# The second layer's FFN down projections as seven products instead of eight

## The chip, the cores and the metric

The kernel runs on one core of one Trainium2 chip. The metric is the device time of one execution in microseconds. Each core has five engines with queues of their own: TensorE (PE, matmuls; PEld, its weight loads), VectorE (DVE), ScalarE (ACT), GpSimd (POOL) and SyncE (SP), which here only issues DMAs. The engines wait for each other, and for transfers, through semaphores. On-chip memory is SBUF (128 partitions); matmuls write PSUM, which has eight banks of 128 x 512 f32.

## What is computed

Two layers of a decoder trunk on 512 tokens of 1024 features. In each, a normed x feeds one wide projection, four token mixers in parallel, their gated sum and an output projection; then comes the feed-forward network (FFN). The change is about the FFN, and about how x is held beside it:

```python
FFN_DIM = ((8 * D_MODEL // 3 + 255) // 256) * 256      # 2816
...
def hybrid_layer(x, ...):
    ...
    x = x + merged @ w_out
    hf = rmsnorm(x, norm_ffn)
    gate, up = jnp.split(hf @ ffn_w_up, 2, axis=-1)
    return x + (jax.nn.silu(gate) * up) @ ffn_w_down
```

All data are f32. The kernel keeps their precision with three matmuls for each product: every operand is split into a high part (rounded to the matmul's format) and a low part (the rest), and high x high, high x low and low x high are summed in PSUM (`mm3`, L267).

## The kernel before

Features are the partitions for most of the kernel: h, x and the hidden values of the FFN lie as chunks of 128 features x 512 tokens. The kernel is written on a framework that allocates buffers from pools, finds the waits itself, and orders each engine's instructions by a schedule of its own; `tc.high_priority` moves instructions forward in that order.

Weights go through `Chunk` (L212): one DMA on SyncE's queue brings up to 2048 columns into a raw buffer (`w_raw`, two of them), and halves of 1024 columns are split into `w_hi` (ScalarE, L224) and `w_lo` (VectorE, L225), three buffers each, with high priority. So a raw buffer is free once VectorE has made its last `w_lo`, and a `w_hi`/`w_lo` buffer once TensorE has done its matmuls.

`ffn` (L1052) runs in two parts, over the first six and the last five of eleven column blocks of 256. For each block, two weight chunks give two gate and two up tiles (96 matmuls of 512 columns, `features`), VectorE scales them out of PSUM (L1075), ScalarE takes the Silu, VectorE multiplies (L1080), and the product is split into `a_hi` (ScalarE) and `a_lo` (L1082). Then the part's share of the down projection follows:

- `residual` (L1014): 256 output features at a time, weights stationary, all 512 tokens moving; the sum is added to x (`xT`, held in SBUF from the mixer's end to the layer's end, L1029). In the first layer's second part it also makes the next layer's h and writes x to memory (L1033). In the second layer's first part, each finished chunk of x is transposed to token order by TensorE and copied by ScalarE (`transposed`, L1058) into `x_tok`.
- `final` (L1037): the second layer's second part, with tokens stationary and 512 columns of weights moving into four banks, one for each block of 128 tokens; VectorE adds each bank to `x_tok` (L1045) and the result goes out.

The mixer (L512) reads x back from memory at its end (L1001) and calls `residual` for the output projection (L1011). PSUM banks come from three groups: `mm` (three), `at` (two) and `tr` (three).

Of the kernel before, what the change touches and what calls it, by code (L numbers as in the profile page):

```python
# [21 lines left out]
P = 128  # L22
# [47 lines left out]
def hybrid_trunk(ctx: ExitStack, tc: tile.TileContext, x, mem, positions, norm_mix, w_in, conv_w,  # L70
# [56 lines left out]
    neg = consts.tile([P, P], F32, name="neg")  # L127
# [139 lines left out]
    def mm3(ps, a, b, first, last):  # L267
        ah, al = a
        bh, bl = b
        pe.matmul(ps, ah, bh, start=first, stop=False)  # L270
        pe.matmul(ps, ah, bl, start=False, stop=False)  # L271
        pe.matmul(ps, al, bh, start=False, stop=last)  # L272

    x_dram = nc.dram_tensor("x_spill", [P, KD, S], F32, kind="Internal").ap()
    kv_dram = [nc.dram_tensor(f"kv{l}", [P, 4, 2, 2, MEM], F32, kind="Internal").ap() for l in range(DEPTH)]
# [23 lines left out]
    def column_means(ps, ones, sq, hi, lo):  # L299
        A(hi, sq, AF.Copy)  # L300
        dve.tensor_sub(lo, sq, f(hi))
        pe.matmul(ps, ones, hi, start=True, stop=False)
        pe.matmul(ps, ones, lo, start=False, stop=True)

    def norm_feature(ssq):
        ps = tr_ps()
        column_means(ps, ones_dr, ssq, *(scratch512(S).bitcast(F32R) for _ in range(2)))
# [173 lines left out]
    ones_dr = consts.tile([P, P], F32R, name="ones_dr")  # L481
    dve.tensor_copy(ones_dr, ones_d)
# [8 lines left out]
    mx, e0, e1, sm, z0 = (small(H4, name=f"lb{i}", bufs=1) for i in range(5))  # L491
# [20 lines left out]
    def mixer(l, h, norms, cm, cf):  # L512
# [174 lines left out]
        with pool_("dsa") as dp:  # L687
# [46 lines left out]
            with pool_("idx") as ip:  # L734
# [83 lines left out]
                def select(t):  # L818
# [12 lines left out]
                    dve.copy_predicated(score[:, t * P:], future, neg)  # L831
# [23 lines left out]
                mgp = cf.enter_context(pool_("mgp", "left"))  # L855
# [142 lines left out]
        res = cf.enter_context(tc.tile_pool(name="res", bufs=1))  # L998
# [13 lines left out]
        return h2, ssq2, xT  # L1012

    def residual(xT, w2d, a, kt, cols, h2, ssq2, gain, spill=False, done=None):  # L1014
        for m0 in range(0, KD, cols // P):
            ws = []
            k0 = 0
            per = 2048 // cols
            while k0 < kt:
                n = min(per, kt - k0)  # L1020
                ws.append((k0, n, wchunk(w2d[k0 * P:(k0 + n) * P, m0 * P:m0 * P + cols], n, cols)))
                k0 += n
            pss = [mm_ps() for _ in range(cols // P)]
            for js in ([range(cols // P)] if m0 + cols // P < KD else [[j] for j in range(cols // P)]):
                for k0, n, w in ws:
                    features(w, a, js, k0, kt, [pss[j] for j in js])
            for j in range(cols // P):
                m = m0 + j
                dve.tensor_add(xT[:, m, :], xT[:, m, :], pss[j])  # L1029
                if h2 is not None:  # L1030
                    h_chunk(h2, ssq2, m, gain(m), xT[:, m, :])
                if spill:
                    nc.scalar.dma_start(x_dram[:, m, :], xT[:, m, :])  # L1033
                if done is not None:
                    done(m)

    def final(x_tok, w2d, a, kt):  # L1037
        for m0 in range(0, D, 512):
            cols = slice(m0, m0 + 512)
            ws = [wchunk(w2d[k0 * P:min(k0 + 4, kt) * P, cols], min(4, kt - k0), 512) for k0 in range(0, kt, 4)]  # L1040
            pss = [mm_ps() for _ in range(MM_BUFS)] + [at_ps()]
            tokens_wide(ws, a, kt, pss)
            for t, ps in enumerate(pss):
                for c in ([cols] if m0 == 0 else [slice(m0 + e, m0 + e + 256) for e in (0, 256)]):
                    dve.tensor_add(x_tok[:, t, c], x_tok[:, t, c], ps[:, c.start - m0:c.stop - m0])  # L1045
                    if m0:
                        q = nc.sync if c.start == m0 else nc.scalar
                        q.dma_start(out[0][t * P:(t + 1) * P, c], x_tok[:, t, c])
            if m0 == 0:
                nc.sync.dma_start(out[0][:, cols].rearrange("(t p) c -> p t c", p=P), x_tok[:, :, cols])  # L1050

    def ffn(l, h, ssq, xT):  # L1052
# [5 lines left out]
        def transposed(m):  # L1058
            ps = tr_ps()
            for t in range(NT):  # L1060
                pe.transpose(ps[:, t * P:(t + 1) * P], xT[:, m, t * P:(t + 1) * P], ident)
            A(x_tok[:, :, m * P:(m + 1) * P], ps.rearrange("p (a b) -> p a b", b=P), AF.Copy)

        with tc.tile_pool(name="ffn", bufs=1) as fp:
            for f0, f1 in parts:
                kt = 2 * (f1 - f0)
                a = (fp.tile([P, 12, S], F32R, name="a_hi")[:, :kt], fp.tile([P, 12, S], F32R, name="a_lo")[:, :kt])
                for fc in range(f0, f1):
                    wg = wchunk(ffn_w_up[l][:, fc * 256:(fc + 1) * 256], KD, 256)
                    wu = wchunk(ffn_w_up[l][:, FF + fc * 256:FF + (fc + 1) * 256], KD, 256)  # L1070
                    gs = [fp.tile([P, S], F32, name="fg", bufs=2) for _ in range(2)]
                    us = [fp.tile([P, S], F32, name="fu", bufs=2) for _ in range(2)]
                    for w, dsts in ((wg, gs), (wu, us)):
                        for dst, ps in zip(dsts, features(w, h, (0, 1))):
                            dve.tensor_mul(dst, ps, r_b)  # L1075
                    for j in range(2):
                        i = 2 * (fc - f0) + j
                        g, u = gs[j], us[j]
                        A(g, g, AF.Silu)
                        dve.tensor_mul(g, g, u)  # L1080
                        A(a[0][:, i, :], g, AF.Copy)
                        dve.tensor_sub(a[1][:, i, :], g, f(a[0][:, i, :]))  # L1082
                wd = ffn_w_down[l][f0 * 256:f1 * 256, :]
                h2 = ssq2 = None
                if last and f1 == n_f:
                    final(x_tok, wd, a, kt)
                    continue
                if f1 == n_f:
                    h2, ssq2 = new_h(), new_ssq()
                if last:  # L1090
                    x_tok = fp.tile([P, NT, D], F32, name="x_tok")
                residual(xT, wd, a, kt, 256, h2, ssq2, lambda c: g_mix(l + 1, c), spill=h2 is not None,
                         done=transposed if last else None)
        return h2, ssq2

    for l in range(DEPTH):
        with ExitStack() as ctx_ffn:
            with ExitStack() as ctx_mix:
                h, ssq, xT = mixer(l, h, (lambda: (norm_token(ssq), norm_feature(ssq))) if l else (lambda: norms),
                                   ctx_mix, ctx_ffn)  # L1100
            h, ssq = ffn(l, h, ssq, xT)
# [29 lines left out]
```

## Time and profile before

| | us |
|---|---|
| median of three runs (2047.14 to 2047.64) | 2047.41 |
| the profiled execution | 2046.88 |
| its span, from the first to the last instruction | 2044.9 |
| ScalarE busy in the span | 1022.0 |
| first matmul on the second layer's hidden values | 1808.48 |
| first matmul of `final` | 1986.36 |
| start of the last matmul | 2040.54 |

How to read it: the page gives each engine's busy time and its share of the span, 40 slices of the span with the busy share in tenths and the clock granted to TensorE, the chain of waits (followed back from the last instruction to what released each step), and groups of like instructions with their count, mean duration and the idle time ahead of them. Stretch views give the same sums for chosen times. A matmul's shown duration (some 390 ns) is longer than the pitch at which matmuls follow each other, since they are pipelined.

### The profile page before, as it was taken

To read this page: it belongs to the slowest core of one execution; us is meant where nothing else is said; L and a number is where in the kernel's file an instruction comes from. 1 tells how busy PE (TensorE), PEld (TensorE's weight loads), DVE (VectorE), ACT (ScalarE), POOL (GpSimd) and SP (SyncE) were. 2 spreads that over 40 slices of the span, in tenths; PEclk is the share of its full clock that TensorE was granted. 3 is DMA by queue.
4 is the path that set the end of the run, shared out by engine and by line. 5 is a ranking of instruction groups with operands and counts; after the bars stand their busy time and mean duration, and the time that the engine had idled before them with its cause. 6 is when DMAs were issued, how large, how long until landed. Compare 5 with 4: busy or idle time off the path is not lost.

```text
span 2044.9 us, 26596 instructions
## 1 busy us (share of the span) xinstructions
PE 2032.3 (99%) x10348; PEld 1714.7 (84%) x10348; DVE 1274.7 (62%) x2519; ACT 1022.0 (50%) x1844; POOL 9.8 (0%) x33
## 2 busy tenths in 40 slices
PE   8999999999999999999999999999999999999999
PEld 8998988888888888888889898888888788888887
DVE  6779998547676544334457889953777654533442
ACT  7653655766665423223355466576766633322231
POOL 0000000000000000000000000000000000000000
PEclk9999999999999999999999999999999999999999
DMA  7623222223233232232243213322222423323222
GB/s 253 219 88 94 68 93 93 64 71 93 83 113 114 87 100 92 93 110 97 88 155 94 88 59 112 93 73 63 83 83 83 144 89 97 103 73 112 93 83 93
DMA packets 187709, 203.79 MB, mean 100 GB/s; under 512 B 4271, under 2 KB 176385, under 8 KB 187457
## 3 DMA queue, kind: packets, MB, share of 16 engines
q1 hardware_dynamic: 183296, 193.04, 29.7%
q10 hardware_dynamic: 4128, 8.93, 1.2%
q8 instruction: 81, 1.33, 0.3%
q14 instruction: 44, 0.35, 0.1%
q0 software_dynamic: 160, 0.13, 0.0%
HBM read 191.60 MB, written 10.49 MB: 99 GB/s over the span
## 4 chain that ended last, share of the span: by engine, by line
PE 98%; DMA 1%; ACT 1%; DVE 1%; issue 0%; SPq 0%; DVEq 0%
PE mm L270 30%; PE mm L271 29%; PE mm L272 29%; PE tr L726 1%; PE tr L720 1%; PE at L697 1%; PE at L696 1%; PE at L272 1%; PE at L270 1%; PE at L271 1%; DMA w_raw<-in_mem_w_kv_dram 1%; PE at L974 0%; PE at L948 0%; PE tr L664 0%; PE tr L765 0%; PE tr L631 0%
## 5 line engine op out<-in xcount | busy, mean ns | idle before, releaser
L270 PE MATMUL mm<-h_hi,w_hi 128*128 128x512 f32 x1664 | 652.0, 393 | 1.0 <-DVE fg L1075 0.4
L225 DVE TENSOR_TENSOR w_lo<-w_raw,w_hi 128x1024 fp32r<-128x1024 f32 (+1 forms) x346 | 419.7, 1214 | 372.3 <-ACT w_hi L97 371.9
L271 PE MATMUL mm<-h_lo,w_hi 128*128 128x512 f32 x1664 | 651.5, 392 | 0.0
L272 PE MATMUL mm<-h_hi,w_lo 128*128 128x512 f32 x1664 | 649.1, 391 | 0.0
L97 ACT ACTIVATE w_hi<-w_raw 128x1024 fp32r<-128x1024 f32 (+1 forms) x346 | 363.3, 1051 | 452.5 <-PE mm L271 406.1
L270 PEld LDWEIGHTS mm<-h_hi,w_hi 128*128 128x128 f32 x1664 | 312.7, 188 | 66.0 <-DVE fg L1075 1.2
L272 PEld LDWEIGHTS mm<-h_hi,w_lo 128*128 128x128 f32 x1664 | 312.6, 188 | 64.2 <-issue 0.2
L271 PEld LDWEIGHTS mm<-h_lo,w_hi 128*128 128x128 f32 x1664 | 312.8, 188 | 63.0 <-issue 1.0
L272 PE MATMUL mm<-w_hi,h_lo 128*128 128x256 f32 (+1 forms) x448 | 128.2, 286 | 0.0
L271 PE MATMUL mm<-w_lo,h_hi 128*128 128x256 f32 (+1 forms) x448 | 127.0, 284 | 0.0
L270 PE MATMUL mm<-w_hi,h_hi 128*128 128x256 f32 (+1 forms) x448 | 127.0, 285 | 0.0
L271 PE MATMUL mm<-a_lo,w_hi 128*128 128x512 f32 x272 | 106.3, 391 | 0.0
L270 PE MATMUL mm<-a_hi,w_hi 128*128 128x512 f32 x272 | 106.0, 390 | 0.0
L272 PE MATMUL mm<-a_hi,w_lo 128*128 128x512 f32 x272 | 105.7, 391 | 0.0
L270 PE MATMUL mm<-y_hi,w_hi 128*128 128x512 f32 x256 | 100.7, 395 | 1.2 <-ACT y_hi L97 1.2
L272 PE MATMUL mm<-y_hi,w_lo 128*128 128x512 f32 x256 | 100.4, 392 | 0.0
L271 PE MATMUL mm<-y_lo,w_hi 128*128 128x512 f32 x256 | 100.3, 392 | 0.0
L272 PEld LDWEIGHTS mm<-w_hi,h_lo 128*128 128x128 f32 x448 | 85.7, 191 | 1.4 <-issue 0.8
L270 PEld LDWEIGHTS mm<-w_hi,h_hi 128*128 128x128 f32 x448 | 85.3, 191 | 1.2 <-issue 0.8
L271 PEld LDWEIGHTS mm<-w_lo,h_hi 128*128 128x128 f32 x448 | 85.6, 191 | 0.6
L97 ACT ACTIVATE a_hi<-fg 128x512 fp32r<-128x512 f32 x44 | 27.8, 633 | 106.8 <-DVE fg L1080 106.8
L97 ACT ACTIVATE prob<-prob,small 128x128 f32<-128x128 f32 (+3 forms) x128 | 69.2, 555 | 15.2 <-DVE small L709 14.6
(370 smaller groups left out, 2958.1 us busy)
## 6 DMA issues: line engine op xcount, KB each, us to landing
w_raw<-in_w_in_dram SPq DMA_DIRECT2D x72, 1024.0 KB, 5.3
w_raw<-in_ffn_w_up_dram SPq DMA_DIRECT2D x44, 1024.0 KB, 5.1
w_raw<-in_w_lift_dram SPq DMA_DIRECT2D x32, 512.0 KB, 3.4
w_raw<-in_ffn_w_down_dram SPq DMA_DIRECT2D x16, 1024.0 KB, 5.4
w_raw<-in_mem_w_kv_dram SPq DMA_DIRECT2D x8, 1024.0 KB, 5.2
w_raw<-in_w_out_dram SPq DMA_DIRECT2D x8, 1024.0 KB, 5.3
w_raw<-in_ffn_w_down_dram SPq DMA_DIRECT2D x10, 512.0 KB, 3.4
kv<-kv ACTq DMA_DIRECT2D x8, 512.0 KB, 6.4
```

The source lines that it names most:

```text
L97: i = act.activation(dst, src, func, **kw)
L225: dve.tensor_sub(lo, raw[:, k:e], f(hi))
L270: pe.matmul(ps, ah, bh, start=first, stop=False)
L271: pe.matmul(ps, ah, bl, start=False, stop=False)
L272: pe.matmul(ps, al, bh, start=False, stop=last)
L696: pe.matmul(ps, q[:, hh, s], k[0][:, :n], start=True, stop=False)
L697: pe.matmul(ps, q[:, hh, s], k[1][:, :n], start=False, stop=True)
L720: pe.transpose(pp[:, (2 * e + i) * P:(2 * e + i + 1) * P], probs[2 * i + e][:, b * P:(b + 1) * P], ident)
L726: pe.matmul(pv[e * HD:(e + 1) * HD, :], vt[:, b, :], pt[:, b, e * 2 * P:(e + 1) * 2 * P], start=b == 0, stop=b == t)
```

## The change

The second layer's down projection is written as a block product with one block fewer. For each pair of hidden chunks (K = 2 x 128), the hidden values are cut into halves by K (the two chunks g0, g1) and by tokens (256 each), and the weights by K and by columns (`C2` = 0:512, `C1` = 512:1024). Seven products of quarter size, whose operands are sums and differences of quarters, replace eight; some stand in several results, and the banks are added to the accumulator `acc` (x in token order) several times.

- `operands` makes from g0 and g1 seven half-token tiles, high and low, for all pairs of a part (six buffers each).
- `down` runs four loops over the pairs. The first and second use four banks; `ba` goes on accumulating over all four loops, `bb` restarts with the second. The second loop makes two differences of weights on VectorE and writes one of them to memory (`t2_spill`, on ScalarE's queue); the fourth reads it back. `evict`, with twice the priority offset of the splits, adds banks to `acc` between the loops.
- `raw_tile` gives every third raw weight tile a third buffer (`w_raw7`).
- The first layer's down projection keeps its eight products (`add_down`), but x isn't held in SBUF: `residual` always writes its chunks to memory, and the FFN fetches them one by one on GpSimd's queue (`x_chunk`) and, in the first layer, writes them back after each part. In the second layer the fetched chunks are transposed during the up projections of blocks 1 to 4 (`x_in`).
- Smaller edits: `neg` has one column and is broadcast, one matrix of ones is dropped and its factor goes into `column_means`, five small tiles share a ring, x and the merged branches leave SBUF with the mixer, the FFN's pool waits tile by tile for reused memory, and `mm3` can pass a flag.

```diff
-    neg = consts.tile([P, P], F32, name="neg")
+    neg = consts.tile([P, 1], F32, name="neg")
...
-    def column_means(ps, ones, sq, hi, lo):
-        A(hi, sq, AF.Copy)
-        dve.tensor_sub(lo, sq, f(hi))
+    def column_means(ps, ones, sq, hi, lo, scale=1.0):
+        A(hi, sq, AF.Copy, scale=scale)
+        dve.scalar_tensor_tensor(lo, sq, scale, f(hi), op0=OP.mult, op1=OP.subtract)
...
+    def add_down(x_chunk, w2d, a, kt, h2, ssq2, gain):
+        for m0 in range(0, KD, 2):
...
+            xs = [x_chunk(m0 + j) for j in range(2)]
...
+            for j, xc in enumerate(xs):
+                m = m0 + j
+                dve.tensor_add(xc, xc, pss[j])
                 if h2 is not None:
+                    h_chunk(h2, ssq2, m, gain(m), xc)
+                nc.scalar.dma_start(x_dram[:, m, :], xc)
...
+    def raw_tile(fp, turn=[0]):
+        turn[0] += 1
+        if turn[0] % 3 == 0:
+            return fp.tile([P, 2048], F32, name="w_raw7")
+        return wpool.tile([P, 2048], F32, name="w_raw", bufs=RAW_BUFS)
+
+    def split(src):
...
+        with tc.high_priority(offset=AHEAD):
+            A(hi, src, AF.Copy)
+            dve.tensor_sub(lo, src, f(hi))
...
+    def operands(fp, g0, g1):
...
+        put(A11, 1, g0[:, :HALF])
+        put(A12, 2, g1)
+        dve.tensor_add(g0[:, HALF:], g0[:, HALF:], g1[:, HALF:])
+        dve.tensor_sub(g0[:, :HALF], g0[:, HALF:], g0[:, :HALF])
+        both = g1.rearrange("p (a b) -> p a b", b=HALF)
+        dve.tensor_sub(both, both, g0[:, None, :HALF].to_broadcast([P, 2, HALF]))
+        put(S2, 2, g0)
+        put(S4, 2, g1)
+        return hi, lo
+
+    def down(fp, w2d, ops, spill, evict):
...
+        ba, bb = [mm_ps(), mm_ps()], [b0, at_ps()]
...
+        for i0 in range(0, n, 2):
...
+            nc.sync.dma_start(raw, w2d[2 * i0 * P:2 * (i0 + m) * P, C1].rearrange("(k p) n -> p k n", p=P))
+            for i in range(m):
+                p1, p2 = split(raw[:, 2 * i:2 * i + 2, :])
+                prod(ba, i0 + i, A11, p1, i0 + i == 0, i0 + i == n - 1)
+                prod(bb, i0 + i, A12, p2, i0 + i == 0, i0 + i == n - 1)
+        evict(ba, 0, C1, 0)
+        evict(bb, 0, C1, 1)
+        for i in range(n):
+            raw = raw_tile(fp)[:, :1536]
+            nc.sync.dma_start(raw[:, :1024], w2d[2 * i * P:(2 * i + 1) * P, :])
+            nc.sync.dma_start(raw[:, 1024:], w2d[(2 * i + 1) * P:(2 * i + 2) * P, C2])
+            with tc.high_priority(offset=AHEAD):
+                dve.tensor_sub(raw[:, 512:1024], raw[:, :512], raw[:, 512:1024])
+                dve.tensor_sub(raw[:, 1024:], raw[:, 1024:], raw[:, 512:1024])
+            p5, p6 = split(raw[:, 512:].rearrange("p (k n) -> p k n", n=512))
+            nc.scalar.dma_start(spill[:, i, :], raw[:, 1024:])
+            prod(ba, i, S2, p6, False, i == n - 1, True)
+            prod(bb, i, S1, p5, i == 0, i == n - 1)
+        evict(ba, 0, C2, 0)
+        evict(bb, 2, C2, 0)
+        for i0 in range(0, n, 2):
...
+            with tc.high_priority(offset=AHEAD):
+                dve.tensor_sub(raw[:, 0::2, :], raw[:, 1::2, :], raw[:, 0::2, :])
+            for i in range(m):
+                p7, p3 = split(raw[:, 2 * i:2 * i + 2, :])
+                prod(ba, i0 + i, S3, p7, False, i0 + i == n - 1, True)
+                prod(bb, i0 + i, S4, p3, False, i0 + i == n - 1, True)
+        evict(ba, 2, C2, 1)
+        evict(bb, 0, C2, 1)
+        for i0 in range(0, n, 2):
...
+            nc.sync.dma_start(raw[:, :m, :], rows[:, i0:i0 + m, 1, C1])
+            nc.sync.dma_start(raw[:, m:, :], spill[:, i0:i0 + m, :])
+            with tc.high_priority(offset=AHEAD):
+                dve.tensor_sub(raw[:, :m, :], raw[:, :m, :], raw[:, m:, :])
+            for i, p4 in enumerate(split(raw[:, :m, :])):
+                prod(ba, i0 + i, A22, p4, False, i0 + i == n - 1, True)
+        evict(ba, 2, C1, 0)
...
+            def x_chunk(m):
+                xc = fp.tile([P, S], F32, name="x_c", bufs=2 if last else 4)
+                nc.gpsimd.dma_start(xc, x_dram[:, m, :])
+                return xc
...
+                    ops.append(operands(fp, *gs))
+                    if fc == 0:
+                        acc = fp.tile([P, NT, D], F32, name="acc")
+                    if 0 < fc < 5:
+                        x_in(2 * fc - 2)
+                        x_in(2 * fc - 1)
...
+                def evict(bank, t0, cols, times):
+                    tail = final and t0 and cols is C1
+                    with tc.high_priority(offset=2 * AHEAD):
+                        for t, ps in enumerate(bank):
+                            for w in (slice(0, 256), slice(256, 512)) if tail else (slice(0, 512),):
+                                c = slice(cols.start + w.start, cols.start + w.stop)
+                                d = acc[:, t0 + t, c]
+                                dve.tensor_add(d, d, ps[:, w])
```

More of the change, by code (lines that the diff above doesn't have):

```diff
@@ L490, in hybrid_trunk @@
     a0, a1 = prm[:, 64:68], prm[:, 68:72]
-    mx, e0, e1, sm, z0 = (small(H4, name=f"lb{i}", bufs=1) for i in range(5))
+    mx, e0, e1, sm, z0 = (small(H4) for _ in range(5))
     dve.tensor_max(mx, a0, a1)
@@ L1029, in residual @@
                 dve.tensor_add(xT[:, m, :], xT[:, m, :], pss[j])
-                if h2 is not None:
[L1031 to L1050, printed above, removed]
@@ L1094, in ffn @@
+                down(fp, wd, ops, t2_dram[:, part], evict)
         return h2, ssq2
     for l in range(DEPTH):
[L1097 to L1101, printed above, removed]
+        with ExitStack() as ctx_mix:
+            h, ssq = mixer(l, h, (lambda: (norm_token(ssq), norm_feature(ssq))) if l else (lambda: norms), ctx_mix)
```

127 lines of the change are left out of this document (80 added, 47 removed).

## The prediction

> **What bounds the kernel now.** First the page's head: how long the span is, which engine fills it, and whether its clock is whole.
>
> ```profile
> span 2044.9 us, 26596 instructions
> ...
> PE 2032.3 (99%) x10348; PEld 1714.7 (84%) x10348; DVE 1274.7 (62%) x2519; ACT 1022.0 (50%) x1844; POOL 9.8 (0%) x33
> ...
> PEclk9999999999999999999999999999999999999999
> ...
> PE 98%; DMA 1%; ACT 1%; DVE 1%; issue 0%; SPq 0%; DVEq 0%
> PE mm L270 30%; PE mm L271 29%; PE mm L272 29%; PE tr L726 1%; PE tr L720 1%; PE at L697 1%; PE at L696 1%; PE at L272 1%; PE at L270 1%; PE at L271 1%; DMA w_raw<-in_mem_w_kv_dram 1%; PE at L974 0%; PE at L948 0%; PE tr L664 0%; PE tr L765 0%; PE tr L631 0%
> ```
>
> TensorE is busy 99% of the span and is 98% of the chain of waits; its idle time in all is 2044.9 - 2032.3 = 12.6 us. So a matmul left out is worth its full pitch, and any new wait of TensorE costs its full length. The pitch comes from the stretch view over the second layer's last down projection (`final`, 240 matmuls), and the stretch before it shows the up projections.
>
> ```profile
> 1911.00:1985.00 74.00, 74.00 (x328) 61.27 (x327) 34.44 (x41) 22.06 (x27) 0.00 (x0) 1.00 0.28 90
> ...
> 1986.30:2040.95 54.65, 54.62 (x241) 1.00 0.23 78
> ```
>
> The columns are length, then busy time and count of TensorE, of its weight loads, VectorE, ScalarE and GpSimd (the second row is TensorE alone), granted clock, DMA share, GB/s. 54.65 / 241 = 0.2268 us per matmul of 512 columns, with no hole. VectorE is 47% busy in the up projections, ScalarE 30%: that is the cover for what the change adds.
>
> **The matmuls removed.** Before, the second layer's down projections are 8 x 12 x 3 = 288 matmuls (part of six pairs of K chunks) and 2 x 4 x 10 x 3 = 240 (part of five): 528. After, each pair takes seven products x 2 token blocks x 3 = 42, times 11 pairs: 462. In the built program TensorE's matmuls go from 10071 to 10005, the same 66 fewer. 66 x 0.2268 = **-15.0 us**, certain as long as TensorE is fed. The 32 transposes of x stay (they move from the down to the up projections), and so do the eight copies out of PSUM, so these moves are 0.
>
> **What is put in their place.** The durations, from the groups over the second layer's FFN and from VectorE's timeline:
>
> ```profile
> L225 DVE TENSOR_TENSOR w_lo<-w_raw,w_hi 128x1024 fp32r<-128x1024 f32 x60 | 73.5, 1225 | 126.6 <-ACT w_hi L97 126.6
> L97 ACT ACTIVATE w_hi<-w_raw 128x1024 fp32r<-128x1024 f32 x60 | 63.7, 1061 | 139.5 <-PE mm L271 111.2 <-PE at L272 19.8 <-PE mm L272 8.5
> ...
> L97 ACT ACTIVATE a_hi<-fg 128x512 fp32r<-128x512 f32 x21 | 13.3, 633 | 52.9 <-DVE fg L1080 52.9
> ...
> L1045 DVE TENSOR_TENSOR x_tok<-x_tok,mm 128x256 f32<-128x256 f32 x6 | 2.3, 418 | 11.1 <-PE mm L272 11.1
> L1045 DVE TENSOR_TENSOR x_tok<-x_tok,mm 128x512 f32<-128x512 f32 x3 | 2.0, 683 | 0.6 <-PE mm L272 0.6
> ```
>
> ```profile
> 1942.44 0.69 DVE L1082 TENSOR_TENSOR a_lo<-fg,a_hi 128x512 fp32r<-128x512 f32 x1 [0.70 <-ACT a_hi L97]
> 1943.05 0.69 DVE L1075 TENSOR_TENSOR fu<-mm,rstd 128x512 f32<-128x512 f32 x1
> 1943.96 1.22 DVE L225 TENSOR_TENSOR w_lo<-w_raw,w_hi 128x1024 fp32r<-128x1024 f32 x1 [0.23 <-ACT w_hi L97]
> 1945.10 0.68 DVE L1080 TENSOR_TENSOR fg<-fg,fu 128x512 f32<-128x512 f32 x1
> ```
>
> Back to back on VectorE a 512-wide subtraction takes 0.61 us (1942.44 to 1943.05) and a 1024-wide one 1.14 (1943.96 to 1945.10); a split of 1024 columns is 1.06 on ScalarE and then 1.14 on VectorE. In the up projections `operands` replaces two 512-wide subtractions by four and three 256-wide ones: 4 x 0.61 + 3 x 0.42 - 2 x 0.61 = +2.5 us per 96 matmuls (21.8 us), 11% more on a VectorE that is 47% busy; ScalarE gets about 1.0 more (633 ns a copy): hidden, 0. If that cover were gone, the projections' banks would be emptied late and up to 2.5 us per step would show.
>
> In the down projections I call the four loops of `down` passes 1 to 4. A tile is one pair's weights (1024 columns, 12 matmuls, 2.72 us; in pass 4, two pairs). With six pairs the passes are 72, 72, 72 and 36 matmuls. VectorE has, in pass 2, 12 new 512-wide subtractions (7.3), six splits (6.8) and four accumulator additions (2.4) = 16.6 us against 16.3 us of matmuls; over all four passes about 50 us against 57. So it is not the bound by amount, but it is full in pass 2, and it takes its instructions in the order that the scheduler wrote. What decides is when each raw buffer is filled. The transfers:
>
> ```profile
> w_raw<-in_ffn_w_down_dram SPq DMA_DIRECT2D x16, 1024.0 KB, 5.4
> w_raw<-in_ffn_w_down_dram SPq DMA_DIRECT2D x10, 512.0 KB, 3.4
> ...
> xT<-x_spill SPq DMA_DIRECT2D x16, 256.0 KB, 5.2
> ...
> mv<-kv SPq DMA_DIRECT2D x8, 256.0 KB, 3.0
> ...
> x_spill<-xT ACTq DMA_DIRECT2D x8, 256.0 KB, 6.2
> ```
>
> ```profile
> 10.00:15.00 5.00, 3.08 (x17) 1.98 (x18) 4.04 (x15) 4.23 (x11) 0.00 (x0) 0.97 1.04 408
> 15.00:20.00 5.00, 5.00 (x32) 5.00 (x32) 2.62 (x13) 4.84 (x11) 0.00 (x0) 0.69 1.08 360
> ...
> 1595.00:1600.00 5.00, 3.83 (x16) 2.47 (x14) 2.87 (x5) 1.14 (x2) 0.00 (x0) 1.00 0.00 0
> ```
>
> A pass 2 tile loads 512 + 256 KB and spills 256 KB: 1.05 MB per 2.72 us is 385 GB/s, while the busiest stretch of the trace moved 408. There are three raw buffers; one is free again when its split is done and its spill has landed. No row has 768 KB: between 3.4 and 5.4 I take 3.4 for the first transfer and 4.4 for both. A 256 KB spill lands in 3.0 us (the kv row, alone) to 6.2 (the x_spill row, beside weight loads).
>
> **The waits, worked through the built order.** Clock 0 is the end of the first part's up projections. VectorE still has the last pair's operands to make, and waits in between for pass 2's first raw buffer, whose subtractions stand among them; the split of pass 1's fourth tile so ends at about 8.5 and of the sixth at 11.4. Only these free the buffers of pass 2's second and third tiles: loaded at 12.0/12.9 and 14.9/15.8, their four subtractions end at 16.5, the second tile's split at 17.6, and only behind it in VectorE's order stands the first accumulator addition (18.3). TensorE is done with pass 1 at 72 x 0.2268 = 16.3 and adds pass 2 onto that same bank: **it waits 2.0 us**. Behind the waiting matmul stands the rest of TensorE's queue, and nothing else can use the time.
>
> Going on in the same way: the split of pass 2's fourth tile stands behind the sixth tile's subtractions, so behind the third buffer's spill and load: 0.2 us (spill 3.0) to 1.9 (spill 6.2). Pass 2 to 3: the first buffer of pass 3 (1 MB, 5.4) is subtracted ahead of the additions, and its split behind two of them: 1.8 to 2.4. Pass 3 to 4: the addition stands behind the third buffer's subtraction: 1.5. First part: 5.5 to 7.8. Second part (five pairs): its additions stand one split earlier, 0.7; pass 2, 0.3; pass 2 to 3, with the split behind all four additions, 2.4 to 5.0; pass 3 to 4, 0.1. That is 3.5 to 6.1. Together 9.0 to 13.9. I take **+10.5**, nearer the lower end because a spill of pass 2 meets loads of 768 KB, a good part of which have landed by then, where the 6.2 row meets 1 MB loads.
>
> The bounds of this cost: below, if the additions never wait for a transfer, each boundary costs the two additions that TensorE cannot run beside, 0.7 us at most, so about 4; above, if both loads take the 5.4 row and every spill the 6.2 row, each of the seven waits grows by another 1.0: 13.9 + 7 = 20.9.
>
> **The clock.** At 15 to 20 us the granted clock is 0.69, after stretches in which TensorE was idle 1.9 us of 5; at 1595 to 1600 it idled 1.17 us and kept 1.00. My waits of 0.7 to 2.4 us lie between these, so I cost the clock at 0 and keep a rival for it: by the row at 15 us every wait might be charged. The Trainium skill, page "TensorE: Matmul & The Clock Gate", section "HAM oscillation — how this bites in real kernels", says that idle gaps of more than about 3.4 us halve the clock. By that rule only a wait at the upper end of the longest one (5.0 us) would be charged, and an estimate from the page's window of 3.4 us at half speed is 1.7 us on the sum.
>
> **First layer, and the rest.** `add_down` fetches x in chunks on GpSimd's queue and writes them back on ScalarE's. A fetch is at most 5.2 us and the write before it 6.2; four buffers let it start one step of 72 matmuls (16.3 us) ahead: hidden, 0. Without that cover each of the eight steps would wait up to 5.2. The 24 further writes of x and 11 spills are issued on ScalarE, which is half idle. `norm_feature`, the narrower `neg` and the pools change no count of instructions on the path. The scheduler also reorders the mixers; the idle time of the whole trace, 12.6 us, shows that little can be won there, and I take 0, with 3 us either way. The end is alike: a last matmul, two 256-wide additions, two transfers.
>
> **Sum.** 2044.9 - 15.0 + 10.5 = 2040.4 span. The profiled run took 2046.88, 2.0 more than its span, which gives 2042.4; the median of the runs shown, 2047.41, lies 0.5 above the profiled run, so **2042.9 us**.
>
> **Rivals.**
> Cover holds: raw buffers come in time, waits of about 4 to 6 us, 2047.4 - 15.0 + 5 = 2037.4. For it: 385 GB/s lies under the 408 that a stretch reached, and VectorE has 7 us to spare. Against: the order puts additions behind work that waits for transfers.
> All given back: spills always at 6.2 and some waits longer, 15 us: 2047.4.
> Slower: the ring of three raw buffers sets the pace of pass 2. Place: VectorE at `down`'s two subtractions, for a buffer whose spill has not landed. Price: the upper bound, 20.9 us, 2047.4 - 15.0 + 20.9 = 2053.3. It decides once load plus spill takes more than about 10 us in the mean, so that the waits exceed 15. For it: the 5.4 and 6.2 rows; against: three buffers, and only three tiles of each pass 2 need a buffer that has just been spilled.
> The clock: each of seven waits costs a spell like that at 15 to 20 us, 0.31 x 5 = 1.55: 7 x 1.55 = 10.9 more, 2053.8. Against it: the 1.17 us hole that cost nothing.
> That the products are not saved at all can be left out: the built order has them.
>
> **How the numbers follow.** A measurement of this kernel can tell about 0.2% (4.1 us) from no change: faster is below 2043.3, slower above 2051.5. The forecast (waits of 7 to 14 us, 2039 to 2046.5) has 0.50, cover holds 0.20, all given back 0.09, the ring 0.16, the clock 0.05. Faster: 0.20 and 0.30 of the forecast's 0.50, whose centre lies just under the bound: 0.50. Slower: the ring and the clock, 0.21. Same: the rest, 0.29. The range reaches from the second rival's lower waits (2036) to the ring (2053); the forecast's own is 2039 to 2046.5.
>
> **What would show it.** Right: TensorE shows 66 matmuls fewer and in each part three holes, the longest at the changes of pass, ended by an accumulator addition or a split on VectorE; the pitch stays 0.227; DMA over 300 GB/s in pass 2; up projections and first layer without new holes. The sum of holes sets the time: about 10 us. Wrong: holes in the first layer ended by x chunks, a granted clock under 1.00 in the passes, or pass 2 stretched evenly (the ring).

## The result, and the profile after

| | before | after |
|---|---|---|
| median, us | 2047.36 (2047.14 to 2047.64, 4 runs) | 2056.01 (2054.34 to 2056.84, 4 runs) |
| the profiled execution's span | 2044.9 | 2052.6 |
| last matmul of the second mixer's output projection starts | 1676.70 | 1683.05 |
| first part of the down projection, first to last matmul | 67.89 | 65.20 |
| second part | 54.17 | 56.01 |

The ratio is 1.0041, 95% interval 1.0029 to 1.0053: slower, by 8.6 us in the medians and 7.7 in the spans. The page of the changed kernel, its head, chain of waits and the down projections' weight loads:

```profile
span 2052.6 us, 26852 instructions
...
PE 2030.9 (99%) x10282; PEld 1703.5 (83%) x10282; DVE 1353.0 (66%) x2634; ACT 1047.7 (51%) x1883; POOL 22.6 (1%) x57
...
PE 93%; DMA 3%; DVE 2%; ACT 1%; issue 1%; SPq 0%; DVEq 0%; ACTq 0%
...
w_raw<-in_ffn_w_down_dram SPq DMA_DIRECT2D x18, 1024.0 KB, 5.5
...
w_raw<-in_ffn_w_down_dram SPq DMA_DIRECT2D x22, 512.0 KB, 4.7
```

TensorE has 66 instructions fewer but is busy only 1.4 us less, where 66 x 0.2268 would be 15.0; its share of the chain falls from 98% to 93%, and what took its place is mostly transfers (1% to 3%) and VectorE (1% to 2%). So there are two losses: matmuls that became slower, and waits. The stretch view of the changed kernel finds the place of each (columns as in the prediction: length, busy and count by engine, granted clock, DMA share, GB/s). The rows are the first layer's FFN, the second layer's first up projections, the 192 matmuls of its output projection on `mg` (the merged mixers' outputs, high and low part), and the two parts of its down projection:

```profile
702.70:1044.00 341.30, 341.12 (x1505) 282.12 (x1504) 151.36 (x178) 104.29 (x125) 6.94 (x13) 1.00 0.36 113
...
1684.50:1812.00 127.50, 127.50 (x580) 105.91 (x579) 71.50 (x95) 50.16 (x69) 3.22 (x6) 1.00 0.37 121
1638.48:1683.05 44.57, 44.57 (x192) 35.85 (x191) 25.56 (x32) 17.47 (x23) 1.06 (x2) 1.00 0.42 137
1817.92:1883.12 65.20, 59.26 (x252) 46.33 (x251) 50.84 (x59) 23.51 (x24) 0.00 (x0) 1.00 0.67 225
1992.15:2048.16 56.01, 51.03 (x210) 39.38 (x209) 42.25 (x53) 17.99 (x19) 0.00 (x0) 0.97 0.62 205
```

The same view of the kernel before, for the same 192 matmuls:

```profile
1633.41:1676.70 43.29, 43.29 (x192) 35.87 (x191) 25.42 (x32) 17.51 (x23) 0.00 (x0) 1.00 0.26 88
```

Both rows are full of matmuls, without a hole, at the whole clock, and yet one takes 1.28 us longer: from first to last start 44.57 / 191 = 233.4 ns a matmul against 43.29 / 191 = 226.7. The matmuls with `y` (one mixer's output, ahead of the merging) as the moving operand slowed too, from 228 to 233 ns start to start in the mean, and no other large group of 512 columns did. With both layers' mixers that comes to 1683.05 - 1676.70 = 6.35 us, all of it ahead of any product that the change leaves out.

The down projections, first to last start, take 65.20 us where 251 pitches of 0.2267 are 56.90, and 56.01 where 209 are 47.38: waits of 8.30 and 8.63 us. What ended TensorE's waits in the first part, from the view of waits (total, times, longest):

```profile
PE mm L270 <- DVE acc L1202: 3.9, 2, 2.3
PE mm L271 <- DVE w_lo L1058: 1.3, 3, 0.5
PE mm L270 <- ACT w_hi L97: 0.7, 1, 0.7
```

and in the second:

```profile
PE mm L270 <- ACT w_hi L97: 4.1, 3, 2.0
PE mm L270 <- DVE acc L1202: 0.6, 2, 0.4
PE mm L271 <- DVE w_lo L1058: 0.2, 1, 0.2
```

In the first part the accumulator additions end most of the waiting, in the second the splits of weights that are late. After the longest wait of the second part the granted clock is half for one window (0.97 in the stretch view), about 1.6 us. The balance: -15.0 for the matmuls, +6.35 ahead, +16.9 in the passes, about -0.6 in small things, is the +7.7 of the spans.

### The profile page after: what moved, and what is told of

Same layout as the page of the kernel before. It is cut to its first block, busy times and chain, and to the rows that moved or that the text cites. A ratio compares the mean times of both kernels' runs of the same rounds, so it can differ in the third digit from the quotient of the medians.

```text
span 2052.6 us, 26852 instructions
## 1 busy us (share of the span) xinstructions
PE 2030.9 (99%) x10282; PEld 1703.5 (83%) x10282; DVE 1353.0 (66%) x2634; ACT 1047.7 (51%) x1883; POOL 22.6 (1%) x57
## 4 chain that ended last, share of the span: by engine, by line
PE 93%; DMA 3%; DVE 2%; ACT 1%; issue 1%; SPq 0%; DVEq 0%; ACTq 0%
PE mm L270 28%; PE mm L271 28%; PE mm L272 28%; DMA w_raw<-in_ffn_w_down_dram 2%; PE tr L725 1%; PE tr L719 1%; PE at L696 1%; DVE w_lo L1058 1%; PE at L695 1%; DMA w_raw<-in_mem_w_kv_dram 1%; ACT w_hi L97 0%; PE at L272 0%; PE at L271 0%; PE at L270 0%; PE tr L663 0%
## 5 line engine op out<-in xcount | busy, mean ns | idle before, releaser
L97 ACT ACTIVATE w_hi<-w_raw 128x1024 fp32r<-128x1024 f32 (+1 forms) x363 | 380.5, 1050 | 443.0 <-PE mm L271 354.5
L225 DVE TENSOR_TENSOR w_lo<-w_raw,w_hi 128x1024 fp32r<-128x1024 f32 (+1 forms) x324 | 392.4, 1212 | 296.1 <-ACT w_hi L97 295.5
L97 ACT ACTIVATE a_hi<-fg 128x512 fp32r<-128x512 f32 (+1 forms) x66 | 39.4, 597 | 113.9 <-DVE fg L1174 97.4
L270 PE MATMUL mm<-a_hi,w_hi 128*128 128x512 f32 x176 | 68.5, 389 | 0.0
L271 PE MATMUL mm<-a_lo,w_hi 128*128 128x512 f32 x176 | 68.5, 389 | 0.0
L272 PE MATMUL mm<-a_hi,w_lo 128*128 128x512 f32 x176 | 68.0, 389 | 0.0
```

The costliest lines, as they stand in the source:

```text
L97: i = act.activation(dst, src, func, **kw)
L225: dve.tensor_sub(lo, raw[:, k:e], f(hi))
L270: pe.matmul(ps, ah, bh, start=first, stop=False, skip_group_check=more)
L271: pe.matmul(ps, ah, bl, start=False, stop=False, skip_group_check=more)
L272: pe.matmul(ps, al, bh, start=False, stop=last, skip_group_check=more)
```

## The experiments

Waits below are, as above, the first-to-last length of a part less its pitches (56.90 and 47.38). A hole is the distance between two matmul starts less one pitch, and a boundary is the change from one pass (one of the four loops of `down`) to the next.

**The slow matmuls.** The small edits take 1152 bytes out of the constants, so the weight parts and h, which lie behind them, move: in the built programs `w_hi` starts at byte 80992 before and 79840 after, 96 and 224 modulo 256. `y` and `mg` are laid out from the other end of memory and stay at 96 modulo 256. Theory A is that this difference slows them. First the changed kernel with one tile more:

```diff
+        shift = mix.tile([P, 32], F32, name="shift")
+        pool.memset(shift, 0.0)
         res = cm.enter_context(pool_("res", "left"))
```

> The changed kernel with 128 bytes more in the mixers' pool, ahead of the lifted outputs' buffers, so that y and mg lie at the same byte address modulo 256 as the weight parts again (both 224; in the changed kernel 96 beside 224, in the kernel before 96 beside 96). Theory A, that a moving operand whose address differs from the stationary one's by 128 modulo 256 makes the matmul slower: the 576 matmuls per layer on y and mg go back from about 233 ns to 227 ns, start to start; 2 x 576 x 5.7 ns = 6.5 us, so the time is about 2049.5 us and the second FFN begins about 6.3 us earlier than in the changed kernel. Rival B, that the slower matmuls come from other work on the memories at that time (transfers of the first layer put on another queue, VectorE writes), or from their order: 2056 us, pitch still 233 ns.

Measured: 2046.73 us (2045.58 to 2048.91), ratio to the kernel before 0.9998, interval 0.9990 to 1.0007. The stretch view, the `mg` row and the two parts:

```profile
1632.72:1676.02 43.30, 43.30 (x193) 35.86 (x191) 25.45 (x32) 17.50 (x23) 1.08 (x2) 1.00 0.42 141
1810.87:1874.22 63.35, 58.93 (x252) 46.41 (x251) 50.87 (x59) 23.51 (x24) 0.00 (x0) 1.00 0.68 231
1983.25:2040.36 57.11, 52.51 (x211) 40.60 (x209) 42.31 (x53) 17.96 (x19) 0.00 (x0) 0.94 0.61 201
```

The matmuls on `mg` take 43.30 us again, with the changed kernel's transfers beside them (0.42 DMA share as in the changed kernel), so it is neither traffic nor order. The projection ends 7.0 us earlier than in the changed kernel (1676.02 against 1683.05); with the first part 1.85 shorter and the second 1.1 longer (by two windows of half clock in place of one), that makes the 7.8 by which the spans differ. Why the parts changed with it is open. The medians differ by 9.3, more than the 6.5 that A had; the changed kernel's profiled run (2054.34) was the fastest of its four. Then the other direction, the kernel before with two of the small edits:

```diff
-    neg = consts.tile([P, P], F32, name="neg")
+    neg = consts.tile([P, 1], F32, name="neg")
...
-    mx, e0, e1, sm, z0 = (small(H4, name=f"lb{i}", bufs=1) for i in range(5))
+    mx, e0, e1, sm, z0 = (small(H4) for _ in range(5))
...
-                    dve.copy_predicated(score[:, t * P:], future, neg)
+                    dve.copy_predicated(score[:, t * P:], future, neg.to_broadcast([P, P]))
```

> The kernel before with two of the small edits alone: the constant neg as one column, and the five lb tiles in the ring of small tiles. The down projections stay plain. The left pools move down by 640 bytes, so the weight parts go from 96 to 224 modulo 256, and y and mg stay at 96. Theory A (addresses): the matmuls on y and mg go from 227 to 233 ns, and the time rises by about 6.3 us to 2053.7. Rival B (other work or the order): within 1 us of 2047.4. Rival C, that the broadcast of neg itself costs something in the selection: the rise stands in the selections, with the pitch of y and mg unchanged.

Measured: 2053.16 us, ratio 1.0028 (1.0017 to 1.0038). The `mg` row:

```profile
1638.36:1682.93 44.57, 44.57 (x192) 35.85 (x191) 25.57 (x32) 17.48 (x23) 0.00 (x0) 1.00 0.25 84
```

The length is that of the changed kernel to the hundredth, and its end lies 6.2 us later than before. Two edits that save 640 bytes and no instruction cost 5.7 us. B falls, and so does C, which had the pitch unchanged. Last, the matmul alone:

> Not the kernel, but its matmul alone: the output is only a copy of x, and all the reference's computation is left out. Stationary tiles of 128x128 and moving tiles of 128x512, FP32R, three matmuls a step as in the kernel, on one core; the stationary side at an address 0 or 128 bytes on, the moving side at 0, 32, 64 ... 480 bytes on, 24 matmuls for each of the 32 pairs; first with nothing else running, then a second time while ScalarE, VectorE and DMA write and read all the while. Theory A (the difference of the two addresses modulo 256 sets the pitch): about 226.5 ns where the difference is 0, about 233 ns where it is 128, with a period of 256, the same for both stationary positions once the difference is taken, quiet or not. Rival A2 (the moving address alone): the slow offsets are the same for both stationary positions. Rival A3 (it is contention with other engines' accesses): no difference in the quiet sweep, one in the second.

The stretch view, one row for 24 matmuls, from the first start of one pair of addresses to that of the next:

```profile
25.37:30.81 5.44, 5.44 (x25) 4.51 (x24) 0.00 (x0) 0.00 (x0) 0.00 (x0) 1.00 0.00 0
30.81:36.42 5.61, 5.61 (x26) 4.50 (x25) 0.00 (x0) 0.00 (x0) 0.00 (x0) 1.00 0.01 3
...
47.53:53.13 5.60, 5.60 (x25) 4.50 (x24) 0.00 (x0) 0.00 (x0) 0.00 (x0) 1.00 0.00 0
136.97:142.43 5.46, 5.46 (x25) 4.50 (x24) 0.00 (x0) 0.00 (x0) 0.00 (x0) 1.00 0.00 0
...
292.94:298.54 5.60, 5.60 (x26) 4.51 (x25) 5.43 (x6) 5.41 (x7) 0.00 (x0) 1.00 1.09 347
315.35:320.82 5.47, 5.47 (x26) 4.50 (x24) 5.30 (x6) 5.31 (x6) 0.00 (x0) 1.00 1.08 347
```

These are, in order: moving less stationary address 0, 32 and 128 bytes with the stationary side at 0; 0 with the stationary side at 128; and there once more, while the other engines and 347 GB/s of transfers run, 128 and 0. The sixteen moving offsets, for each stationary position and with or without traffic, give the same pitch at the same difference modulo 256, within 1 ns:

| difference modulo 256, bytes | 0 | 32 | 64 | 96 | 128 | 160 | 192 | 224 |
|---|---|---|---|---|---|---|---|---|
| ns a matmul | 227 to 228 | 233.5 | 229.3 | 233.9 | 233.5 | 234 | 233.5 | 233.1 |

A holds; the moving address alone (A2) and contention (A3) fall.

**The waits.** The first idea was VectorE's order:

```diff
+    def behind(i, made):
+        for m in made:
+            tc.add_manual_dep(i.ins, m.name, order, reason="additions first")
...
-        evict(ba, 0, C1, 0)
+        made = evict(ba, 0, C1, 0)
...
-                dve.tensor_sub(raw[:, 512:1024], raw[:, :512], raw[:, 512:1024])
+                i1 = dve.tensor_sub(raw[:, 512:1024], raw[:, :512], raw[:, 512:1024])
+                behind(i1, made if i > 1 else [])
```

and so at the other two boundaries.

> The changed kernel with an order given to VectorE at the three boundaries of each down projection: the subtractions of the next pass, from its second tile of weights on (third pass: from the first; fourth: from the second), are issued behind the additions that free the first pair of accumulators. No instruction is added or taken away. Theory D, that the holes at the first and the third boundary (2.50 and 1.72 us in part 1, 1.54 in part 2) come from subtractions ahead of the additions on VectorE: these fall to under 1 us each, the total of the waits in the two parts from 16.9 to about 13 us, and the time to about 2052.5. Rival E, that the transfers alone decide (the weights are late whatever the order): the hole only moves to the next split, and the time stays within 0.7 us of 2056.

Measured: 2058.98 us, ratio 1.0059 (1.0046 to 1.0071): slower. TensorE's waits in the first part:

```profile
PE mm L270 <- ACT w_hi L97: 2.4, 1, 2.4
PE mm L270 <- DVE acc L1210: 2.2, 3, 1.0
PE mm L271 <- DVE w_lo L1058: 1.7, 1, 1.7
```

The additions now cost 2.2 instead of 3.9 (first boundary 2.50 to 2.06 in two pieces, third 1.72 to 0.59), but the second boundary, whose subtractions were put back, grew from 1.6 to 4.4. Two windows of half clock came in each part. The waits are 10.6 and 12.2; without the clock (four windows, 1.6 each) 16.4, where the changed kernel has 15.3. In the second part the third boundary's hole, which D had under 1 us, grew from 1.5 to 2.0, and one inside the second pass from 0.9 to 2.1. D falls for the three boundaries together, and E's form, "the hole only moves", holds; that the clock would make it dearer was in neither.

> Both edits together. If A and D hold and add up: about 2046, below the kernel before by about 1.4 us. If only A holds: 2049.5; only D: 2052.5; neither: 2056.

Measured: 2052.60 us (1.0015 to 1.0033): A's gain (6.4 against e3) and e3's loss (5.9 against e1) add up. That it is the number expected for "only D" is chance: A holds here, and the order costs time.

Then what the weights are late for. Without the writes of t2:

```diff
-            nc.scalar.dma_start(spill[:, i, :], raw[:, 1024:])
...
-            nc.sync.dma_start(raw[:, m:, :], spill[:, i0:i0 + m, :])
+            nc.sync.dma_start(raw[:, m:, :], rows[:, i0:i0 + m, 1, C2])
```

> The changed kernel without the writes that put the second pass's combinations (t2) into DRAM; the fourth pass reads as many bytes of the weights in their place, so what is subtracted there is not what the reference needs. Theory R (the holes from the second pass to the third come from the three raw buffers: each is held until its t2 write has landed, and the next load stands behind it on SP): the loads of the third pass are issued earlier, the hole at that boundary falls from 2.18 to under 1 us in part 2 and from 1.6 to under 0.8 in part 1, no window of half clock follows, and the waits of part 2 go from 8.6 to about 5 us. Rival V (VectorE has too much in front of the split): the holes stay within 0.5 us of what they were. The hole from the first pass to the second (2.50 us in part 1) changes in neither.

Measured in one run: 2055.32 us; waits 8.2 and 9.2, with a window of half clock in each part. Without these two, 14.2 are left of 15.3. In the second part the hole of 2.18 became 0.72 and another of 3.2 three matmuls later, so it moved; R's 5 us for this part and its whole clock did not come, and V's unchanged holes did not either. In the changed kernel the weight loads of the third pass (L1119) waited mostly for t2 writes, from the view of waits of SP's queue over the second part:

```profile
SPq L1205 <- DVE acc L1202: 18.3, 8, 6.2
SPq L1105 <- DVE w_lo L1058: 11.5, 3, 10.4
SPq L1119 <- DMA t_spill<-w_raw: 10.8, 3, 6.5
```

and without these writes, for splits:

```profile
SPq L1105 <- DVE w_lo L1058: 22.4, 5, 10.4
SPq L1204 <- DVE acc L1201: 16.6, 6, 5.7
SPq L1130 <- DVE w_lo L1058: 12.9, 3, 8.1
SPq L1118 <- DVE w_lo L1058: 6.7, 3, 2.6
```

The write was the last thing to hold a buffer, not the only one. (The largest line of the first view, output writes that wait for additions, is no cause here: the load behind them, at 2011.62, still had 0.9 us to wait for a t2 write.) Without the weight subtractions (L1108, L1109, L1121 and L1134 left out):

> The changed kernel without its four kinds of weight subtractions on VectorE (some 20 to 24 instructions of 0.69 to 1.23 us a part); the passes multiply the weights as loaded, so the output is another. Loads, writes and splits stay. Theory V: VectorE's amount of work makes the holes, so those at the first and the third boundary fall from 2.50, 1.72 and 1.54 to under 0.5 us, that at the second from 2.18 to under 1.2, and the waits of the two parts from 16.9 to under 7 us in all. Theory R: the boundary from the second pass to the third still has a hole of at least 1.5 us in part 2, because its load stands behind the t2 write, and the waits stay over 10 us in all.

Measured in one run: 2047.72 us, with no window of half clock in the two parts:

```profile
1818.24:1878.92 60.68, 57.70 (x252) 46.89 (x251) 36.87 (x42) 23.62 (x24) 0.00 (x0) 1.00 0.72 241
1987.95:2041.57 53.62, 48.80 (x210) 38.84 (x209) 30.36 (x37) 18.00 (x19) 0.00 (x0) 1.00 0.64 214
```

That is waits of 3.8 and 6.2, in all 10.0 where V said under 7 and R over 10. In the first part the first and third hole are 0.54 each, about what V has, and the second boundary has 2.37, more than the 1.6 of the changed kernel; in the second part 1.49 inside the second pass, 2.11 at the second boundary and 1.37 at the third are left. So without VectorE's subtractions some 5 us of the 15.3 go, most of them in the first part, and the rest stays. Last, more buffers, where the memory has room for them: in the second part h is read no more, and two raw tiles can lie there.

```diff
-    def raw_tile(fp, turn=[0]):
+    def raw_tile(fp, extra, turn=[0]):
         turn[0] += 1
-        if turn[0] % 3 == 0:
+        n = turn[0] % (5 if extra else 3)
+        if n == 0:
             return fp.tile([P, 2048], F32, name="w_raw7")
+        if n > 2:
+            return f(state.tile([P, KD, S], F32R, name=("h_hi", "h_lo")[n - 3], bufs=1)[:, :4]).rearrange(
+                "p a b -> p (a b)")
```

> The changed kernel with the 128 bytes (as in e1) and, in the second part's down projection alone, five raw buffers in place of three: the two further ones lie where h was, which nothing reads any more. No other instruction is changed. Theory R: in part 2 the holes inside the second pass and at the second boundary, 9.4 us of waits and slow clock with e1, fall to about 3 us (what the accumulators cost at the boundaries), and the time from 2046.7 to about 2041, under the kernel before; part 1 stays at 6.4 us. Rival T (the transfers' rate decides, 218 GB/s moved there already): the loads are issued earlier but land as late, and the time is within 1 us of 2046.7. Rival V (VectorE): the same, the splits come no earlier.

Measured: 2043.09 us (2042.41 to 2045.07), ratio 0.9980 (0.9971 to 0.9990). The two parts:

```profile
1811.49:1876.49 65.00, 60.39 (x253) 47.67 (x252) 51.01 (x60) 23.40 (x24) 0.00 (x0) 0.97 0.66 229
1985.51:2036.95 51.44, 48.66 (x211) 38.76 (x209) 40.50 (x51) 17.66 (x19) 0.00 (x0) 1.00 0.60 213
```

The second part's waits fall from 9.7 (57.11 in e1) to 4.1; of these 5.7, 3.2 are the two windows of half clock that are gone, and 2.5 are waits. The holes inside the second pass, at the second and at the third boundary are 0.8, 0.55 and 0.54, and the one at the first grew from 0.6 to 1.55. Of the gain of 5.7 the time keeps 3.6, since a window of half clock fell into the first part here; R had 2041. Where the weights come from shows on SP's queue. In the changed kernel the last load of the second pass (L1105) and the first of the third (L1119) are issued at

```profile
2011.62 0.34 SPq L1105 DMA_DIRECT2D w_raw<-in_ffn_w_down_dram  x1
2012.01 0.46 SPq L1106 DMA_DIRECT2D w_raw<-in_ffn_w_down_dram  x1
2015.99 0.38 SPq L1119 DMA_DIRECT2D w_raw<-in_ffn_w_down_dram  x1
```

The last lands some 5.7 us later, VectorE subtracts at 2021.80, and TensorE, out of work at 2022.3, goes on at 2024.31. With five buffers (the second pass ends 6.7 us earlier here) they go out at

```profile
1996.21 0.33 SPq L1111 DMA_DIRECT2D h_hi<-in_ffn_w_down_dram  x1
...
1997.95 0.38 SPq L1125 DMA_DIRECT2D h_lo<-in_ffn_w_down_dram  x1
```

which is 18 us ahead of the end of the second pass (2015.6), not 6. T and V had the time within 1 us of 2046.7, and it is 3.6 lower; the passes go faster, at 213 GB/s where e1 had 201. So neither is what makes these holes. R holds with a correction: it is the number of buffers, not the t2 write alone, that makes the loads late.

With the weights early, the order can help at the one boundary where nothing is late behind it:

```diff
-        evict(ba, 2, C2, 1)
+        made = evict(ba, 2, C2, 1)
...
-                dve.tensor_sub(raw[:, :m, :], raw[:, :m, :], raw[:, m:, :])
+                i1 = dve.tensor_sub(raw[:, :m, :], raw[:, :m, :], raw[:, m:, :])
+                for e in made if i0 > 2 else []:
+                    tc.add_manual_dep(i1.ins, e.name, order, reason="additions first")
```

> The kernel of e8 with the order on VectorE at one boundary only: the fourth pass's subtractions, from its second tile on, stand behind the additions that free the accumulators of its first products. In e3, where all three boundaries were ordered, this one fell from 1.72 to 0.59 us in part 1. Theory D4 (here nothing is late behind it, since the fourth pass has half the products of the others on PE... and its loads are early): part 1's hole at the third boundary falls from 1.73 to about 0.6, part 2's stays at 0.54, and the time falls by about 1 us, to 2042. Rival E (the work only moves): a new hole of about 1 us inside the fourth pass of part 1, and the time within 0.4 us of 2043.1.

> The kernel of e8 once more, beside e9 on the same chip. In e8 one window of half clock fell into part 1, behind the hole of 2.4 us between its first and second pass (56% of that window idle), where e1 had none at 55%. If that is the place of the window boundary in the run and nothing of the kernel, a profile of this kernel may be without it, and part 1 then takes 63.3 us as in e1 in place of 65.0; the median stays at 2043.1 within 0.7 us.

Measured: e9 2041.71 us, ratio 0.9973 (0.9963 to 0.9984); e8's kernel again 2042.83, 0.9979 (0.9971 to 0.9988), with a window of half clock in the first part again. e9's parts:

```profile
1811.91:1874.74 62.83, 58.76 (x252) 46.49 (x251) 51.18 (x59) 23.51 (x24) 0.00 (x0) 1.00 0.71 238
1983.77:2035.64 51.87, 48.93 (x210) 38.76 (x209) 40.51 (x51) 17.67 (x19) 0.00 (x0) 1.00 0.62 211
```

The third boundary's hole in the first part fell from 1.73 to 0.59 as D4 said, and no hole came inside the fourth pass; one inside the second grew from 0.2 to 1.0, and the second part is 0.5 longer than in e10. So 0.7 of the 1.1 us gained at the boundary is lost inside the second pass, where neither D4 nor E had it. The medians differ by 1.1 us, but the intervals of the ratios overlap, and the profile's 2.2 us in the first part are partly the missing clock window. e9 is the fastest kernel here, 5.5 us under the one before and 14.3 under the changed one.

## Why the prediction was wrong

It said 2042.9 with a range of 2036 to 2053; the result is 2056.0. Its steps:

- **Matmuls removed, -15.0: right.** 10348 to 10282 instructions, and the passes' pitch stayed at 0.2267.
- **Up projections and `operands` hidden, transposes 0, first layer 0: right.** The rows at 1684.50 (127.50 of 127.50 us busy) and 702.70 (341.12 of 341.30, before 340.60 of 340.80) have no new holes. The end after the last matmul is 4.4 us in both.
- **The failed step: "change no count of instructions on the path ... and I take 0, with 3 us either way".** That the count stays was right; that a matmul's pitch stays with it was assumed. The edits moved addresses, and 1152 matmuls ahead of the down projections lost 5.5 ns each, 6.35 us, twice the allowance. e1 and e2 show that this is the cause, in both directions. Nothing in the trace of before announced it, but the addresses could have been compared.
- **The second failed step: waits, +10.5, "nearer the lower end".** They were right in kind and too small: 15.3, and 1.6 of half clock:

| boundary | said, part 1 | measured | said, part 2 | measured |
|---|---|---|---|---|
| first to second pass | 2.0 | 2.5 | 0.7 | 0.9 |
| inside the second | 0.2 to 1.9 | 0.7 | 0.3 | 1.1 |
| second to third | 1.8 to 2.4 | 1.6 | 2.4 to 5.0 | 2.4 |
| third to fourth | 1.5 | 1.7 | 0.1 | 1.5 |

 The first part's boundaries were right within 0.5. The second part's were too short inside the second pass and at the third boundary, both ended by splits: I let the buffers there come in time. The reason given for the lower end was that the loads beside a t2 write have in good part landed by then. In the second part the three loads of the third pass (at 2015.99, 2017.28 and 2024.28) waited for t2 writes issued at 2011.05, 2012.38 and 2017.84, which puts these writes at 4.9, 4.9 and 6.4 us, in the upper half of the 3.0 to 6.2 that I had or over it. (The one write of the first part whose landing the trace shows took 3.2; the kv row that I took 3.0 from is a read.) The two loads of a tile were right in the first part (4.4 for both, measured from 1830.42 to 1834.80), but of three tiles asked for within 3.3 us in the second (from 2000.48) two had their second load landing 6.4 and 7.4 us after its issue. The rest, some 2.9 us, is a split of the first pass (0.4) that I did not have and many small pieces, among them about 0.1 us more for the first matmul after each hole.
- **The clock at 0: wrong by 1.6.** It fell to half behind one wait of 2.02 us. So a granted clock under 1.00 in the passes, one of the prediction's signs of being wrong, came. The rule quoted from the Trainium skill, page "TensorE: Matmul & The Clock Gate", section "HAM oscillation — how this bites in real kernels", by which gaps over about 3.4 us do that, does not agree with this: the gap was shorter. Its rival, a charge for each of seven waits, was wrong too.
- **The rivals.** The ring of three raw buffers was the nearest. e8 shows its mechanism in the second part, where two buffers more take 5.7 us off, 3.2 of them clock; its price of 20.9 was too high, and its place (the t2 write) was not the only one, by e6. "DMA over 300 GB/s in pass 2" was not reached: 275 and 293.

Either of the two errors alone, 6.35 or 6.4 (16.9 less 10.5), would have left the time at 2049.3, inside the range.

Open: what more buffers would do to the first part, and what is left of its first boundary (2.3 us in e9, ended by additions). h is alive there, so its memory can't serve, and it wasn't tried.

## What to carry to other kernels

A change that takes a few hundred bytes from one pool moves every tile behind it: compare the addresses of the operands that meet in a matmul before costing "small edits" at nothing, and keep them equal modulo 256. Where several passes follow each other on the same buffers, count how far ahead of its use each load can be issued, with everything that still holds its buffer; an order of additions and subtractions only moves the hole while weights are late. Saved matmuls are worth their pitch only if the engine that now prepares their operands is not late at any boundary.

## What the runs showed of the hardware

- An FP32R matmul of 128 x 512 follows the one before after 227 to 228 ns where moving and stationary operand have the same address modulo 256, and after 229 to 234 ns otherwise, with no other engine at work too (e5; no other shape or type was tried). That is up to 3% of TensorE's time.
- The clock goes by fixed windows. In all profiles its changes lie on a grid of 3.413 us: in the changed kernel it rises at 17.31 and falls at 2024.35, 588 windows later. That agrees with the Trainium skill, "TensorE: Matmul & The Clock Gate", section "What's actually happening", which has a free-running window of 3413 ns. What decides in the FFN is TensorE's busy time in one window, not the length of a gap. Three windows of the changed kernel (length, TensorE busy, granted clock last but two):

```profile
1833.20:1836.61 3.41, 1.93 (x9) 1.27 (x7) 3.00 (x4) 1.54 (x2) 0.00 (x0) 1.00 0.86 269
2020.94:2024.35 3.41, 1.39 (x7) 0.80 (x6) 2.55 (x4) 1.15 (x2) 0.00 (x0) 1.00 0.95 359
2024.35:2027.76 3.41, 3.17 (x7) 2.03 (x8) 3.41 (x5) 0.85 (x1) 0.00 (x0) 0.50 0.47 161
```

 The longer hole, 2.34 us from 1835.1, lies across two windows and leaves the first 1.93 us busy: nothing follows. The hole of 2.02 us lies in one window, which is busy 1.39, and the next runs at half. In e1 a window busy 1.54 was followed by half clock and one of 1.55 was not:

```profile
1827.79:1831.20 3.41, 1.55 (x7) 1.31 (x8) 3.10 (x5) 1.06 (x1) 0.00 (x0) 1.00 0.90 301
2012.11:2015.52 3.41, 1.54 (x8) 0.76 (x6) 3.11 (x5) 1.71 (x2) 0.00 (x0) 1.00 0.95 365
2015.52:2018.93 3.41, 3.07 (x7) 1.97 (x7) 3.41 (x4) 0.76 (x2) 0.00 (x0) 0.50 0.45 154
```

 In e8 1.50 was followed by it, in e9 1.56 was not. In the eleven profiles of the two kernels, e1 to e4 and e6 to e10, behind the first 20 us, every window at the whole clock that was busy 1.54 us or less was followed by half clock, and none that was busy 1.55 or more. So the limit here lies near 1.55 of 3.41 us (45%), as far as modelled ends of matmuls allow. In the first 20 us, where the matmuls are shorter, it does not come out: the window of the changed kernel from 7.07 is busy 2.02, and the next runs at half. A half window can bring a second one: behind the one busy 3.07 of e1 came another, behind the one busy 3.17 of the changed kernel none. A window at half clock costs about 3.41 x (1 - 227 / 427) = 1.6 us, at the 427 ns that matmuls take then.
